# Dense experts of a PEER layer: z through one PSUM bank in two pieces, five output tiles kept in PSUM

## The chip, the cores and the metric

The kernel runs on one core of a Trainium2 chip. The metric is device time in microseconds (us). Three timed runs of the kernel before took 3194.96, 3195.38 and 3200.4 us; the median is 3195.38 us. One more execution was profiled, and every number from the trace is of that one.

## What is computed

The reference is one encoder block on 1024 tokens of width 1024: RMSNorm, a gated mixer of differential attention and a short convolution, then a PEER layer and a last RMSNorm. The change lies in the PEER layer:

```python
q = (xc @ w_query).reshape(c, PEER_HEADS, 2, PEER_HALF_DIM)
sc = jnp.einsum('chpd,hpnd->chpn', q, sub_keys)
s1, i1 = lax.top_k(sc[:, :, 0], 16); s2, i2 = lax.top_k(sc[:, :, 1], 16)
cand = s1[..., :, None] + s2[..., None, :]          # 256 candidates of a head
top, pos = lax.top_k(cand, 16)                      # 16 experts of 16384 for a token and head
g = jax.nn.softmax(top, axis=-1)
a = gelu(jnp.einsum('chkd,cd->chk', expert_u[eidx], xc))
out = jnp.einsum('chk,chkd->cd', g * a, expert_v[eidx])
```

Each token thus takes 8 x 16 = 128 of 128 x 128 experts, and an expert is one row of u and one row of v.

## The kernel before

The 1024 tokens are eight tiles of 128. The experts of the first five tiles (640 tokens, `GB`) are computed densely: for all 16384 experts, with a weight that is zero where a token did not choose the expert. The experts of the other three tiles are gathered: for each of 128 choices of a tile, an indirect DMA fetches one row of u and v for every token (`uvt`, four buffers), VectorE multiplies u with the token and sums (line 746), ScalarE takes the GELU and the weight (lines 748 and 749), and VectorE adds weight times v to `acc` (line 755): 3 x 128 = 384 such steps.

The dense part goes over the 128 rows of the expert grid, 128 experts in a row, in the loop of line 974. Matmul operands are split into a rounded high part and a low part (`split`: a cast on ScalarE, a subtraction on VectorE), and a product takes three matmuls: high x high, high x low, low x high (`passes`). A row i does this:

- `expert_in(i)`: u of the row is loaded (`raw`, a ring of three buffers that u, v and, at the end, h share) and split (`uh`, `uhl`). z is u times the 640 normed tokens: eight steps of 128 features, three matmuls each, for each of two halves of 320 tokens, so 48 matmuls of 320 columns. Both halves are one PSUM tile of two banks with one buffer. One GELU of 640 columns (line 929) makes `pr` (one buffer), VectorE multiplies it with the weights (line 930), and the product is split into `ph` and `phl`.
- `expert_out`: the output of the preceding block of two rows (`BLK`): ten tiles of 128 tokens x 512 features, six matmuls of 512 columns each (two rows, three matmuls). In program order five of the ten tiles follow z of the next block's first row, five z of its second row. The four tiles of the first two token tiles (`NR`) stay in four PSUM banks over all 128 rows (`held`). The other six go through two banks (`pout`), and VectorE adds each to `hacc` in SBUF (line 957), which starts from the residual h.
- `expert_v(i)`: v of the row is loaded and split into `vh` and `vhl` (three buffers each).

After the loop, `finish_rows` adds h to the held tiles, takes the last RMSNorm of the five token tiles and writes them out; each one needs one more buffer of the ring `raw` for the squares (`yo`). What is left of the gathers comes after that.

Eight PSUM banks are in use: two for z, two for `pout`, four for `held`.

The order on each engine isn't the program's order. The framework runs through the instructions with estimated durations, gives each engine what is ready by them, the earlier in program order first, and fixes that order; on the chip each engine runs its list in order and waits by semaphores. So z matmuls of one row and output matmuls of the preceding block lie mixed in the trace. The gathers and the top-k of the last tiles are generators that put in a step after so many us of matmul work (`tick`; `GATHER` is 2.0 us), and have their place in the program order from there.

## Time and profile before

| | |
|---|---|
| median of three runs | 3195.38 us |
| profiled execution | 3191.78 us |
| its span, first to last instruction | 3190.0 us |
| TensorE, VectorE, ScalarE, GpSimd busy | 94%, 83%, 41%, 29% of the span |
| granted TensorE clock, mean | 0.978 of full speed |
| matmuls of z, of the output | 6144, 3840 |
| dense GELUs, adds to hacc, gather steps | 128, 384, 384 |

Times in the rows are microseconds from the start of the span, unless marked ns. PE is TensorE's matmul, DVE is VectorE, ACT is ScalarE, POOL is GpSimd, SP is the engine that issues most DMAs. Matmuls are pipelined: the duration of one is longer than the time from its start to the next one's start. L905 is line 905 of the kernel; `out<-in` names what is written and read. What stands after `<-` in brackets is what ended the idle time before an instruction.

### The profile page before, as it was taken

The numbers are of one execution on the slowest core, as the hardware profiler recorded it, in microseconds if no ns is written. First come the engines' busy times: TensorE is split into PE (matmuls) and PEld (weight loads), VectorE is DVE, ScalarE is ACT, GpSimd is POOL, SyncE is SP. The second block draws the span as 40 slices with busy tenths as digits, with TensorE's granted clock in tenths as the row PEclk, the third lists the DMA queues.
The fourth block names the chain that finished last, engine by engine and source line by source line (L and its number), as shares of the span: only waits on it lengthen the run. The fifth ranks groups of instructions, "written<-read, shape, count | busy, mean of one in ns | idle before, by whom it ended". The sixth has DMA issues, their size and how long they took to land.

```text
span 3190.0 us, 45907 instructions
## 1 busy us (share of the span) xinstructions
PE 3012.1 (94%) x17551; PEld 2761.0 (87%) x17551; DVE 2646.3 (83%) x4665; ACT 1302.9 (41%) x2344; POOL 923.5 (29%) x716
## 2 busy tenths in 40 slices
PE   7999999898989879799999999999999999999994
PEld 6799998798988869789989989899889999999993
DVE  5442466378999996799999999999999999999898
ACT  3322364335567766533333333333333333333332
POOL 2310000035344444223222222223332323333333
PEclk9999999999999989899999999999999999999997
DMA  5451232555444375779878888888889999898887
GB/s 180 145 182 67 83 113 80 199 172 213 146 172 157 144 260 196 255 249 333 316 277 321 316 299 309 295 316 293 313 328 343 340 341 348 326 347 325 328 336 281
DMA packets 237549, 801.11 MB, mean 251 GB/s; under 512 B 18832, under 2 KB 123280, under 8 KB 174096
## 3 DMA queue, kind: packets, MB, share of 16 engines
q0 software_dynamic: 64704, 442.53, 37.5%
q1 hardware_dynamic: 152592, 305.30, 27.8%
q10 hardware_dynamic: 20032, 50.34, 4.1%
q8 instruction: 138, 2.26, 0.3%
q14 instruction: 83, 0.68, 0.1%
HBM read 714.74 MB, written 83.36 MB: 250 GB/s over the span
## 4 chain that ended last, share of the span: by engine, by line
PE 56%; DVE 17%; issue 11%; DMA 8%; POOL 4%; ACT 3%; SPq 0%; ACTq 0%; POOLq 0%; DVEq 0%
PE z L905 17%; PE pout L905 10%; PE held L905 6%; PE pq L228 4%; PE pg L228 4%; POOL uvt L739 3%; PE ph L228 3%; DMA uvt<-in_uv,idx 3%; DVE acc L755 2%; PE py L228 2%; PE pw L695 2%; DVE uvt L746 2%; DVE ms L714 1%; PE pv L228 1%; PE pk L228 1%
## 5 line engine op out<-in xcount | busy, mean ns | idle before, releaser
L739 POOL DMA_INDIRECT uvt<-in_uv,idx x384 | 528.1, 1375 | 1288.5 <-DVE acc L755 1011.0
L905 PE MATMUL z<-actTh,uh 128*128 128x320 f32 x2048 | 636.3, 311 | 5.5 <-ACT pr L929 4.5
L905 PE MATMUL z<-actTh,uhl 128*128 128x320 f32 x2048 | 636.5, 311 | 1.1 <-DVE uhl L898 1.1
L905 PE MATMUL z<-actTl,uh 128*128 128x320 f32 x2048 | 635.3, 310 | 0.0
L746 DVE SCALAR_TENSOR_TENSOR uvt<-uvt,hng 128x1024 f32<-128x1024 f32 x384 | 468.0, 1220 | 41.1 <-DMA uvt<-in_uv,idx 40.3
L755 DVE SCALAR_TENSOR_TENSOR acc<-uvt,wt,acc 128x1024 f32<-128x1024 f32 x381 | 487.8, 1280 | 1.3 <-ACT wt L749 1.2
L905 PEld LDWEIGHTS z<-actTh,uh 128*128 128x128 f32 x2048 | 386.0, 188 | 20.5 <-ACT pr L929 8.6
L905 PEld LDWEIGHTS z<-actTl,uh 128*128 128x128 f32 x2048 | 386.2, 189 | 10.1
L905 PEld LDWEIGHTS z<-actTh,uhl 128*128 128x128 f32 x2048 | 386.8, 189 | 8.5 <-DVE uhl L898 2.2
L905 PE MATMUL pout<-vh,ph 128*128 128x512 f32 x768 | 302.5, 394 | 23.2 <-ACT ph L896 15.0
L905 PE MATMUL pout<-vhl,ph 128*128 128x512 f32 x768 | 301.1, 393 | 0.0
L905 PE MATMUL pout<-vh,phl 128*128 128x512 f32 x768 | 300.5, 391 | 0.0
L718 POOL TENSOR_TENSOR o<-ms,wtr 128x512 f32<-128x512 bf16 x160 | 203.0, 1311 | 262.1 <-PE pw L695 123.4
L748 ACT ACTIVATE wt<-zt 128x1 f32<-128x1 f32 x384 | 77.0, 201 | 493.3 <-DVE uvt L746 493.0
L957 DVE TENSOR_TENSOR hacc<-pout,hacc 128x512 f32<-128x512 f32 x384 | 259.4, 681 | 19.6 <-PE pout L905 19.1
L185 DVE TENSOR_TENSOR wl<-wr,wh 128x2048 fp32r<-128x2048 f32 x66 | 157.9, 2392 | 117.7 <-ACT wh L184 117.7
L896 ACT CAST uh<-raw 128x1024 fp32r<-128x1024 f32 x128 | 134.3, 1049 | 193.5 <-DMA raw<-in_uT 187.9
L184 ACT CAST wh<-wr 128x2048 fp32r<-128x2048 f32 x74 | 141.0, 1907 | 168.9 <-DMA wr<-in_wq 31.6
L695 PE MATMUL pw<-o,o 128*128 128x128 f32 x1280 | 169.1, 284 | 41.2 <-POOL o L718 17.6
L695 PEld LDWEIGHTS pw<-o,o 128*128 128x128 f32 x1280 | 161.1, 198 | 49.3 <-issue 25.6
L905 PE MATMUL held<-vhl,ph 128*128 128x512 f32 x512 | 199.6, 391 | 0.0
L720 ACT CAST o<-ms 128x512 f32<-128x512 bf16 x160 | 179.6, 1138 | 38.8 <-DVE ms L714 26.0
(290 smaller groups left out, 6673.5 us busy)
## 6 DMA issues: line engine op xcount, KB each, us to landing
raw<-in_uT SPq DMA_DIRECT2D x128, 512.0 KB
raw<-in_uv SPq DMA_DIRECT2D x128, 512.0 KB
w_d<-wbuf ACTq DMA_DIRECT2D x20, 2048.0 KB
wt<-w_d SPq DMA_DIRECT2D x32, 1280.0 KB
wr<-in_wcols SPq DMA_DIRECT2D x28, 1024.0 KB
wr<-in_wq SPq DMA_DIRECT2D x24, 1024.0 KB
xt<-in_x SPq DMA_DIRECT2D x16, 512.0 KB
q_d<-qt POOLq DMA_DIRECT2D x32, 256.0 KB
```

The source lines that it names most:

```text
L184: A.copy(out=op[0][sl], in_=src)
L185: lo.tensor_sub(op[1][sl], src, op[0][sl].bitcast(F32))
L228: PE.matmul(pd, lhsT=l[a], rhs=r[b], start=i == 0 and j == 0, stop=i == n - 1 and j == len(c) - 1)
L695: PE.matmul(pw[:, u, :], lhsT=o2[:, t + u, :], rhs=o1[:, t + u, :], start=True, stop=True)
L718: PL.tensor_tensor(out=o1.rearrange("p t i -> p i t"), in0=ms[:, 0], in1=w[:, ts].unsqueeze(1).broadcast_to(sh), op=ALU.mult)
L720: A.copy(out=o2.rearrange("p t i -> p i t"), in_=ms[:, 1])
L739: PL.indirect_dma_start(out=t[:], out_offset=None, in_=uv, in_offset=bass.IndirectOffsetOnAxis(ap=sels[c][1][:, k:k + 1], axis=0))
L746: V.scalar_tensor_tensor(u, u, 1.0, st[c], op0=ALU.mult, op1=ALU.mult, accum_out=zt)
L755: V.scalar_tensor_tensor(st["acc"], v, wt, st["acc"], op0=ALU.mult, op1=ALU.add)
L896: A.copy(out=hi, in_=t)
L905: PE.matmul(ps, lhsT=lhs[k][a], rhs=rhs[k][b], start=first and k == 0 and j == 0, stop=last and k == n - 1 and j == 2)
L957: V.tensor_add(hacc[:, t - NR, ds], ps, hacc[:, t - NR, ds])
```

## The change

z of a row is no longer one tile of two banks. Each half of 320 tokens gets its own tile in one bank with one buffer, and its own GELU into its half of `pr`. Output tiles of the preceding block come after the GELU of the first half (`fill(0)`) and after the split of the product (`fill(1)`), and so four times in a block: three, two, three and two tiles. The bank that becomes free holds a fifth output tile: the first five of the ten (both halves of token tiles 0 and 1 and the first half of token tile 2) stay in PSUM, five are added to `hacc`. Token tile 2 is now half resident and half moving: its half of `hacc` starts from zero, and `finish_rows` adds both to h, which it reads back. The order of tiles alternates moving and resident.

```diff
-NR = 2
+NR = 5
@@ the pools of the last stage @@
-    hacc = hp.tile([P, NB - NR, D], F32, name="hacc")
-    held = [[ps_r.tile([P, 512], F32, name=f"held{t}{hf}") for hf in range(2)] for t in range(NR)]
+    tiles = [(t, hf) for t in range(NB) for hf in range(2)]
+    resident, moving = tiles[:NR], tiles[NR:]
+    hacc = hp.tile([P, len(moving), 512], F32, name="hacc")
+    held = [ps_r.tile([P, 512], F32, name=f"held{j}") for j in range(NR)]
@@ expert_in @@
-    def expert_in(i):
+    def expert_in(i, fill):
...
-        hs = halves(GB)
-        z = ps_z.tile([P, 2, 512], F32, name="z", tag="z")[:, :len(hs), :hs[0][1]]
-        for j, (c0, cn) in enumerate(hs):
-            passes(z[:, j, :], us, [(hh[:, k, c0:c0 + cn], hl[:, k, c0:c0 + cn]) for k in range(KD)], cn)
         p = dn.tile([P, GB], F32, name="pr", tag="pr", bufs=1)
-        A.activation(p.rearrange("p (h c) -> p h c", h=len(hs)), z, AF.Gelu)
+        for c0, cn in halves(GB):
+            z = ps_z.tile([P, cn], F32, name="z", tag="z")
+            passes(z, us, [(hh[:, k, c0:c0 + cn], hl[:, k, c0:c0 + cn]) for k in range(KD)], cn)
+            A.activation(p[:, c0:c0 + cn], z, AF.Gelu)
+            if c0 == 0:
+                fill(0)
         V.tensor_mul(p.rearrange("p (c t) -> p c t", t=WT), p.rearrange("p (c t) -> p c t", t=WT),
                      wts[b][:, :, i % WB, :])
-        return split(p, "ph", PHB, [P, GB], V)
+        ph = split(p, "ph", PHB, [P, GB], V)
+        fill(1)
+        return ph
@@ order of the output tiles, and expert_out @@
     order = []
-    while resident or moving:
-        for q in (moving, resident):
-            if q:
-                order.append(q.pop(0))
+    for j in range(max(len(moving), len(resident))):
+        order += moving[j:j + 1] + resident[j:j + 1]
+    slots = 2 * BLK
+    cuts = [-(-len(order) * j // slots) for j in range(slots + 1)]

     def expert_out(pv, vv, part, first, last):
-        n = len(order) // BLK
-        for t, hf in order[part * n:(part + 1) * n]:
+        for t, hf in order[cuts[part]:cuts[part + 1]]:
...
-            if t < NR:
-                passes(held[t][hf], lhs, rhs, 512, first, last)
+            if (t, hf) in resident:
+                passes(held[resident.index((t, hf))], lhs, rhs, 512, first, last)
             else:
                 ps = ps_v.tile([P, 512], F32, name="pout", tag="v")
                 passes(ps, lhs, rhs, 512)
-                V.tensor_add(hacc[:, t - NR, ds], ps, hacc[:, t - NR, ds])
+                to = hacc[:, moving.index((t, hf)), :]
+                V.tensor_add(to, ps, to)
@@ finish_rows @@
-            if t < NR:
-                y = raw_rows(h_d[rows, :])
-                for hf in range(2):
-                    ds = slice(hf * 512, (hf + 1) * 512)
-                    V.tensor_add(y[:, ds], held[t][hf], y[:, ds])
-            else:
-                y = hacc[:, t - NR, :]
+            y = raw_rows(h_d[rows, :]) if (t, 0) in resident else hacc[:, moving.index((t, 0)):moving.index((t, 0)) + 2, :]
+            y = y if (t, 0) in resident else y.rearrange("p j c -> p (j c)")
+            for hf in range(2):
+                ds = slice(hf * 512, (hf + 1) * 512)
+                if (t, hf) in resident:
+                    V.tensor_add(y[:, ds], held[resident.index((t, hf))], y[:, ds])
+                elif (t, 0) in resident:
+                    V.tensor_add(y[:, ds], hacc[:, moving.index((t, hf)), :], y[:, ds])
@@ the loop over rows @@
     for i in range(NK + BLK):
+        b, part = i // BLK - 1, i % BLK
+        prev = pv[:BLK], vv[:BLK]
+
+        def fill(j):
+            if b >= 0:
+                expert_out(*prev, 2 * part + j, b == 0, b == NK // BLK - 1)
+
         if i < NK:
-            pv.append(expert_in(i))
-        b, part = i // BLK - 1, i % BLK
-        if b >= 0:
-            expert_out(pv[:BLK], vv[:BLK], part, b == 0, b == NK // BLK - 1)
-            if part == BLK - 1:
-                pv, vv = pv[BLK:], vv[BLK:]
+            pv.append(expert_in(i, fill))
+        else:
+            fill(0)
+            fill(1)
+        if b >= 0 and part == BLK - 1:
+            pv, vv = pv[BLK:], vv[BLK:]
...
         if i == 1:
-            for t in range(NR, NB):
-                SP.dma_start(out=hacc[:, t - NR, :], in_=h_d[t * P:(t + 1) * P, :])
+            for j, (t, hf) in enumerate(moving):
+                if (t, 0) in resident:
+                    V.memset(hacc[:, j, :], 0.0)
+                else:
+                    SP.dma_start(out=hacc[:, j, :], in_=h_d[t * P:(t + 1) * P, hf * 512:(hf + 1) * 512])
```

## Rows read from the trace of the kernel before

**Rows 1.** The page's first part: busy time, share of the span and instructions.

```profile
PE 3012.1 (94%) x17551; PEld 2761.0 (87%) x17551; DVE 2646.3 (83%) x4665; ACT 1302.9 (41%) x2344; POOL 923.5 (29%) x716
```

**Rows 2.** Stretches: length, busy us (instructions) by engine, clock, DMA share, GB/s.

```profile
core 0: us, PE busy (x) PEld busy (x) DVE busy (x) ACT busy (x) POOL busy (x), PEclk, DMA share, GB/s
1400.00:2400.00 1000.00, 990.32 (x5483) 893.47 (x5482) 960.84 (x1551) 340.95 (x690) 289.54 (x207) 1.00 0.85 307
2600.00:3000.00 400.00, 400.00 (x2245) 365.82 (x2244) 367.65 (x465) 141.39 (x295) 124.77 (x88) 1.00 0.90 332
```

**Rows 3.** Chain that ended last, 2900 to 3190 us: start, length, engine and line.

```profile
2937.44 5.91 PE z L905 x40
...
3093.54 1.38 PE pout L905 x6
...
3098.81 2.95 PE held L905 x13
...
3144.74 1.20 DVE hacc L957 x2
```

**Rows 4.** TensorE in order of time, its last matmuls: start, length, instruction.

```profile
3145.40 0.50 PE L905 MATMUL pout<-vh,ph 128*128 128x512 f32 x1 [1.68 <-DVE hacc L957]
...
3148.07 0.39 PE L905 MATMUL pout<-vh,phl 128*128 128x512 f32 x1
```

**Rows 5.** Stretches of line 755 alone: accumulations of gathered experts on VectorE.

```profile
1400.00:2400.00 1000.00, 252.50 (x197) 1.00 0.85 307
...
3150.00:3190.00 40.00, 11.55 (x9) 0.53 0.71 262
```

**Rows 6.** Groups, 1200 to 3190 us: busy us, mean ns | idle before, releasers.

```profile
L755 DVE SCALAR_TENSOR_TENSOR acc<-uvt,wt,acc 128x1024 f32<-128x1024 f32 x381 | 487.8, 1280 | 1.3 <-ACT wt L749 1.2
...
L957 DVE TENSOR_TENSOR hacc<-pout,hacc 128x512 f32<-128x512 f32 x384 | 259.4, 681 | 19.6 <-PE pout L905 19.1
...
L896 ACT CAST uh<-raw 128x1024 fp32r<-128x1024 f32 x128 | 134.3, 1049 | 193.5 <-DMA raw<-in_uT 187.9 <-PE z L905 2.7 <-DVE sv L588 2.5
...
L896 ACT CAST ph<-pr 128x640 fp32r<-128x640 f32 x128 | 93.2, 729 | 163.3 <-DVE pr L930 162.3 <-issue 0.8
L929 ACT ACTIVATE pr<-z 128x640 f32<-128x640 f32 x128 | 90.0, 703 | 227.4 <-PE z L905 204.6 <-DVE phl L898 19.8 <-DVE uvt L746 2.7
...
L169 POOL TENSOR_TENSOR r_h<-m_h,mhalf 128x1 f32<-128x1 f32 x5 | 5.7, 1135 | 0.6 <-DVE m_h L167 0.5
```

**Rows 7.** ScalarE in order of time: start, length, instruction, wait before it.

```profile
1348.97 0.72 ACT L896 CAST ph<-pr 128x640 fp32r<-128x640 f32 x1 [13.14 <-DVE pr L930]
...
1363.19 0.71 ACT L929 ACTIVATE pr<-z 128x640 f32<-128x640 f32 x1 [1.20 <-PE z L905]
...
2342.78 0.71 ACT L929 ACTIVATE pr<-z 128x640 f32<-128x640 f32 x1 [2.53 <-DVE phl L898]
...
2525.79 0.71 ACT L929 ACTIVATE pr<-z 128x640 f32<-128x640 f32 x1 [3.86 <-PE z L905]
...
3097.47 0.71 ACT L929 ACTIVATE pr<-z 128x640 f32<-128x640 f32 x1 [5.22 <-PE z L905]
...
3155.13 1.06 ACT L174 ACTIVATE yo<-raw 128x1024 f32<-128x1024 f32 x1 [6.23 <-DMA out<-raw]
```

**Rows 8.** VectorE in order of time: the ends of the same four chains.

```profile
1369.43 0.81 DVE L898 TENSOR_TENSOR phl<-pr,ph 128x640 fp32r<-128x640 f32 x1
...
2349.23 0.81 DVE L898 TENSOR_TENSOR phl<-pr,ph 128x640 fp32r<-128x640 f32 x1
...
2531.19 0.81 DVE L898 TENSOR_TENSOR phl<-pr,ph 128x640 fp32r<-128x640 f32 x1
...
3103.11 0.81 DVE L898 TENSOR_TENSOR phl<-pr,ph 128x640 fp32r<-128x640 f32 x1
```

**Rows 9.** TensorE's waits, 1340 to 3125 us: total us, times, longest.

```profile
PE z L905 <- ACT pr L929: 2.2, 4, 0.9
```

**Rows 10.** ScalarE's waits, 1400 to 2300 us, same columns.

```profile
ACT uh L896 <- DMA raw<-in_uT: 136.1, 54, 7.4
```

**Rows 11.** SP's queue in order of time, 3138 to 3190 us.

```profile
3150.76 13.98 SPq L971 DMA_DIRECT2D out<-raw  x2
```

More of the change, by code (lines that the diff above doesn't have):

```diff
@@ L936, in expert_v @@
         return split(vr, "vh", VHB, [P, D], V)
-    resident = [(t, hf) for t in range(NR) for hf in range(2)]
-    moving = [(t, hf) for t in range(NR, NB) for hf in range(2)]
     order = []
-    while resident or moving:
-        for q in (moving, resident):
-            if q:
-                order.append(q.pop(0))
+    for j in range(max(len(moving), len(resident))):
+        order += moving[j:j + 1] + resident[j:j + 1]
+    slots = 2 * BLK
+    cuts = [-(-len(order) * j // slots) for j in range(slots + 1)]
     def expert_out(pv, vv, part, first, last):
-        n = len(order) // BLK
-        for t, hf in order[part * n:(part + 1) * n]:
+        for t, hf in order[cuts[part]:cuts[part + 1]]:
             ds = slice(hf * 512, (hf + 1) * 512)
```

## The prediction

> **What bounds the kernel now.** I read the busy shares first, then the stretches of the last stage, its groups, its waits, and the two ends of the chain that runs through one row. Over the whole run TensorE is busy 94% and VectorE 83% [rows 1]. The change lies in the dense-expert stage, the last 1850 us. There both engines are nearly full: from 1400 to 2400 us TensorE is busy 99.0% and VectorE 96.1%, from 2600 to 3000 us 100% and 91.9%, at a granted clock of 1.00, the higher of its levels (2.4 GHz) [rows 2].
>
> Busy is not pace, so I count matmuls. A steady z matmul takes 5.91/40 = 0.148 us, a pout one 1.38/6 = 0.230, a held one 2.95/13 = 0.227 [rows 3]. A row needs 48 of z and 30 of output: 7.09 + 18 x 0.230 + 12 x 0.227 = 13.95 us. From 2600 to 3000 us 2245 matmuls ran in 400 us, 0.178 each: that is this floor. From 1400 to 2400 us 5483 ran in 1000 us, where the same pace gives 5612 [rows 2]. The 129 missing ones x 0.178 = 23 us are all that TensorE loses there (a few per cent of the records can be missing, so this is an upper value). So TensorE sets the pace, VectorE is close behind it, and after TensorE's last matmul, which ends at 3148.5 us [rows 4], the span goes on to 3190.0: a tail of 41.5 us. In the tail stand nine of the 384 accumulations of the gathered experts [rows 5], and the finish of the output rows.
>
> **The change, part by part.** The sum is made against the profiled execution: 3191.78 us, 1.78 around its span; the median of the three timed runs is 3.6 higher.
>
> *TensorE's work.* Same matmuls, same shapes: 48 of 320 columns and 30 of 512 a row. Three pout tiles a row become 2.5; pout and held differ by 0.003 us a matmul, so 0.
>
> *VectorE's work.* One of ten tiles of a block leaves the copy to SBUF: 64 adds go. One is listed at 0.681 us [rows 6], but consecutive adds overlap, two in 1.20 us [rows 3], so 64 x 0.60 = 38 us of VectorE, 0.30 a row. Added: one memset of 128x512 (under one such add, 0.7 us) and two adds at the end. Not on the path by itself; it counts where VectorE holds up the end, below.
>
> *ScalarE's work.* The GELU of 640 columns takes 0.703 us; casts of 1024 and 640 columns take 1.049 and 0.729 [rows 6], 0.00083 us a column, so a GELU of 320 is 0.703 - 0.267 = 0.44 us. Twice that is 0.17 more a row, 22 us in all, on an engine that is busy 34% [rows 2]: hidden. SP's queue gets four loads of 256 KB in place of three of 512 KB at the start, and one more 512 KB read of h at the end (below).
>
> *The wait that is added.* Now a row's z pieces pass through one bank: piece 2 waits for the GELU of piece 1, and that GELU writes into "pr", of which there is one buffer, so it also waits until the split of the preceding row's product (phl) is done. Behind a late GELU on ScalarE stand the casts ph, vh and uh and the gathers' wt; behind TensorE's piece 2 stand the next output tiles. The cover is output tiles: slots of 3, 2, 3, 2 tiles, 4.11 us between the pieces and 2.74 after them. Measured from GELU to end of phl, the chain takes 10.2 us on average over the 70 rows from 1363 to 2350 us (7.1 in the first, 7.3 in the last), and 6.2 over the 42 rows from 2526 to 3104 us (6.2 in the first, 6.5 in the last) [rows 7, 8]; 37 of the 70 lie over 9.5. The new loop from GELU to GELU is that chain less 0.26, plus 0.44 for the first GELU and 24 x 0.148 = 3.55 for the second piece: 13.9 us on average in the first group and 9.9 in the second, without handovers. Against a row of 13.95 the second has 4 us of room, the first none. Handovers TensorE to ScalarE and back have no row of their own; the bound is 0 to 0.4 us each.
>
> Does a loop of 13.9 us slow the first 70 rows? Mostly the chain is long there because VectorE is late, with queued gather and top-k work in front of it, and nobody waits: TensorE waited 2.2 us for a GELU in the whole stage [rows 9]. If TensorE is held up, VectorE gets less to do and catches up. But ScalarE also stands 136 us (54 times) before a uh cast whose weights have not landed [rows 10], and a GELU behind that cast now has 3 to 4 us of cover where it had 6.9. The bounds for the 70 rows: -23 us (all that TensorE loses is won, because VectorE has 0.30 us a row less to do), and +95 us (every excess over 9.5 us in those 37 rows stalls TensorE). I take +5: what VectorE is relieved of about pays for the late casts. For the 56 rows behind them I take +2, because the loop has 4 us of room; the bounds are 0 and 28, the second as if one late cast of the earlier kind (136/54 = 2.5 us) came through in every fifth row.
>
> The Trainium skill, "PSUM — Partial Sum Buffer", "Summary: rules for kernel authors", speaks against one bank: an engine should read a bank other than the one that matmuls are writing. By that alone each of the 256 pieces would pay its GELU, 256 x 0.44 = 113 us. The trace of before has the same exclusion once a row (one z tile, one buffer) and shows 2.2 us for it, because output tiles lie between; whether 2.74 us of them still suffice no row shows.
>
> *Start.* Rows 0 and 1 have no output tiles to put between. Before, z of row 1 was finished while ScalarE stood 13.1 us for the first weights [rows 7]; now piece 2 of row 1 waits for the GELU that starts after that and comes out behind it: 3.55 + 0.44 = +4 us.
>
> *Last block.* Five tiles with a copy instead of six, evenly spaced: the last pout tile waited 1.7 us for its bank [rows 4]; -1.
>
> TensorE's last matmul thus moves by 4 + 5 + 2 - 1 = +10.
>
> *Tail.* A gathered expert costs VectorE a product and an accumulation over 128x1024 elements, the second 1.28 us [rows 6], the first of the same form; each overlaps its neighbour by 0.08 as the adds do, so 2.4 us. 38 us of VectorE are 16 of them. From 1400 to 2400 us they ran at 19.7 in 100 us [rows 5] with VectorE full, so there, with half of the adds that go, eight are won, and two more in the 10 us of delay: the nine late ones come before or shortly after the last matmul. What then ends last is the finish. Three output row tiles instead of two now read h back through the three-buffer "raw" ring, and each next one waits until the preceding one is written: 1.06 square [rows 7] + 1.14 power on POOL [rows 6] + 1.28 scaling (the accumulation's form) + 4.4 write (the write issued at 3150.76 released the next square at 3155.13 [rows 7, 11]) = 7.9 us each. The first starts some 8 us before the last matmul, since its two tiles are done before the last five; after two whole turns come the third row's 3.5, two rows that need no h and one write: -8 + 1.2 of adds + 2 x 7.9 + 3.5 + 2 x 1.28 + 4.4 = 19.5 us. With two gathered experts in between, 4.8, it is 24, the value I take; the ends are 18 and 41.5. 24 - 41.5 = -18 rounded.
>
> Sum: +10 - 18 = -8: 3183.8 in the profiled execution, and with the 3.6 us 3187.
>
> **The rivals.**
>
> *A, better: the freed VectorE time goes to TensorE.* For it: 0.30 us a row is more than the 23/70 = 0.33 us a row that is lost, nearly. Then 4 - 23 + 0 - 1 - 18 = -38: 3157.
>
> *B, the loop through z's one bank and "pr" closes (slower).* Place: rows 2 to 71, while the top-k and the gathers fill VectorE. It decides from the point where GELU to end of phl exceeds 13.95 - 3.55 - 0.44 - about 0.5 of handovers = 9.5 us. For it: the 10.2 us average and the 54 late casts. Against: the wait is elastic, and steady rows behind have 6.2. Price: a third to all of the 95 us, +32 to +95, so with the other terms +19 to +82; at half, 4 + 48 + 2 - 1 - 18 = +35: 3230. The rule of the Trainium skill's "PSUM — Partial Sum Buffer" ("Summary: rules for kernel authors") bears on the bank's half of this place; no term here is taken from it.
>
> *C, the tail stays.* The gathers hang on their four buffers and on DMA, 85 to 90% busy [rows 2], not on VectorE. For it: from 2600 to 3000 us VectorE had 8% to spare [rows 2], and nine accumulations were late all the same. Then +10 and no -18, or half of it: +1 to +10, 3196 to 3205.
>
> **How the numbers follow.** The forecast (3177 to 3196 as its own range) gets 0.42, A 0.22, B 0.26, C 0.10. From no change a measurement of this kernel can tell about 0.2%, 6.4 us: faster is below 3189, slower above 3201.8. The forecast lies 0.25 faster and 0.17 same; A is faster; B slower; C is split 0.04 and 0.06. Faster 0.47, same 0.21, slower 0.32. The range 3155 to 3235 reaches from A's value to just beyond the middle of B.
>
> **What would show it.** Right: hacc adds 320 instead of 384; TensorE's waits for a GELU below some 20 us from 1400 to 2400 us, and over 5480 matmuls there; the last matmul within 3140 to 3165 us; a tail near 24 us whose last links are squares and writes of rows, with no accumulation of the gather behind the first of them. B would show as z waiting for pr tens of us long before 2350 us and hardly after it, with a row period over 14.5 us. C would show as gathers still at 20 in 100 us and a tail near 40. The forecast is wrong in its main step if rows 2 to 71 take over 14.5 us or under 13.95 each, and in its second if the tail is not between 18 and 32 us.

## The result, and the profile after

The changed kernel takes 3328.43 us (median of four runs, 3317.97 to 3335.12), the kernel before 3195.17 us in the same comparison. The ratio is 1.0416, 95% interval 1.038 to 1.0452: 4.2% slower, where -0.3% was forecast. The profiled execution took 3325.73 us, its span 3324.0 us, 134.0 us more than before.

The page's first part and two stretches of the last stage, the lines that answer to [rows 1, 2]:

```profile
PE 3060.3 (92%) x17551; PEld 2775.1 (83%) x17551; DVE 2619.4 (79%) x4604; ACT 1320.1 (40%) x2472; POOL 943.4 (28%) x716
```

```profile
1400.00:2400.00 1000.00, 909.31 (x4835) 797.95 (x4834) 933.99 (x1509) 331.52 (x753) 325.71 (x225) 0.98 0.88 316
2600.00:3000.00 400.00, 389.13 (x2146) 351.29 (x2147) 362.48 (x457) 137.35 (x319) 132.33 (x92) 1.00 0.93 339
```

From 1400 to 2400 us 4835 matmuls ran instead of 5483, and from 2600 to 3000 us 2146 instead of 2245. VectorE, which lost 64 adds, is less busy over the whole run. Not so in the rows of the grid from 2 to 48: between their products it is busy 15.8 us of a row of 16.8, before 13.7 of 14.2, because its list has 3.46 accumulations of gathered experts from one product to the next instead of 2.74, and more of the top-k (counted in the timelines; the framework made that list). With this list such a row takes at least 15.8 us. TensorE waits more. Its waits from 1340 to 3125 us, the view of [rows 9] (there 2.2 us for the GELU):

```profile
PE z L907 <- ACT pr L930: 41.6, 58, 3.1
PE pout L907 <- ACT ph L898: 40.4, 25, 11.2
PE pout L907 <- DVE phl L900: 26.1, 19, 4.3
PE pout L907 <- DVE hacc L960: 21.4, 15, 4.1
```

z waits for the GELU in its bank, and the output tiles that were to cover this wait need a product (ph, phl) that is itself late. The page's groups, where [rows 6] has the same ones:

```profile
L907 PE MATMUL pout<-vh,phl 128*128 128x512 f32 x640 | 253.9, 397 | 26.2 <-DVE phl L900 26.1
L898 ACT CAST uh<-raw 128x1024 fp32r<-128x1024 f32 x128 | 134.4, 1050 | 330.5 <-PE z L907 322.3
L960 DVE TENSOR_TENSOR hacc<-pout,hacc 128x512 f32<-128x512 f32 x320 | 214.7, 683 | 56.2 <-PE pout L907 55.6
```

The adds to hacc are 320 now, as said. The cast of uh waited 187.9 us for its weights before; now it waits 322.3 us for z matmuls, which free its buffer. Weights are no longer late, rows are.

One row shows the loop. ScalarE, VectorE and TensorE of the changed kernel in order of time (start, length, instruction, and in brackets the wait before it):

```profile
1698.77 1.05 ACT L898 CAST uh<-raw 128x1024 fp32r<-128x1024 f32 x1 [0.21 <-PE z L907]
1699.72 0.43 ACT L930 ACTIVATE pr<-z 128x320 f32<-128x320 f32 x1
...
1705.62 0.72 ACT L898 CAST ph<-pr 128x640 fp32r<-128x640 f32 x1 [0.21 <-DVE pr L933]
1708.75 0.44 ACT L930 ACTIVATE pr<-z 128x320 f32<-128x320 f32 x1 [2.41 <-DVE phl L900]
```

```profile
1701.29 1.28 DVE L755 SCALAR_TENSOR_TENSOR acc<-uvt,wt,acc 128x1024 f32<-128x1024 f32 x1
1702.48 1.22 DVE L900 TENSOR_TENSOR uhl<-raw,uh 128x1024 fp32r<-128x1024 f32 x1
1703.62 1.22 DVE L746 SCALAR_TENSOR_TENSOR uvt<-uvt,hng 128x1024 f32<-128x1024 f32 x1
...
1704.76 0.82 DVE L933 TENSOR_TENSOR pr<-pr,wt 128x640 f32<-128x640 f32 x1
...
1707.84 0.82 DVE L900 TENSOR_TENSOR phl<-pr,ph 128x640 fp32r<-128x640 f32 x1
```

```profile
1698.57 0.31 PE L907 MATMUL z<-actTh,uhl 128*128 128x320 f32 x1
...
1700.20 0.42 PE L907 MATMUL z<-actTh,uh 128*128 128x320 f32 x1 [0.63 <-ACT pr L930]
...
1703.71 0.31 PE L907 MATMUL z<-actTh,uhl 128*128 128x320 f32 x1
1706.40 0.80 PE L907 MATMUL pout<-vh,ph 128*128 128x512 f32 x1 [2.38 <-ACT ph L898]
1706.99 0.63 PE L907 MATMUL pout<-vhl,ph 128*128 128x512 f32 x1
1707.41 0.63 PE L907 MATMUL held<-vh,ph 128*128 128x512 f32 x1
1707.84 0.63 PE L907 MATMUL held<-vhl,ph 128*128 128x512 f32 x1
...
1709.85 0.40 PE L907 MATMUL held<-vh,ph 128*128 128x512 f32 x1
1710.08 0.40 PE L907 MATMUL held<-vhl,ph 128*128 128x512 f32 x1
...
1712.83 0.31 PE L907 MATMUL z<-actTh,uh 128*128 128x320 f32 x1
```

Read it across. The last matmul of a row's piece 2 starts at 1698.57; the uh cast, freed by its end as the GELU is, stands before the GELU. The GELU ends at 1700.15, VectorE comes to the product only at 1704.76, behind gathered experts and uhl, and ends phl at 1708.66. Meanwhile piece 1 of the next row is ready (1704.0), but its GELU may not write pr before 1708.75. TensorE can't start piece 2, and the output tiles it has instead need ph, so it stands 2.38 us. They then lie in front of piece 2, which starts 3.6 us after its bank is free.

So I set out the loop from one GELU of a first piece to the next, averaged over rows 2 to 47 from such rows of the timeline: GELU 0.44, until piece 2 starts 2.09, piece 2 3.76, until its GELU 1.19, GELU 0.43, until VectorE's product 3.82, product to cast 0.85, cast to the end of phl 4.16, until the next GELU 0.14. The sum is 16.88 us, the row period there. The last term says that it is closed: in 40 of the 46 rows the next GELU starts within 0.3 us of the end of phl, in the other six at most 1.13 us behind it. In rows 84 to 125 the same terms give 14.47 us (VectorE's shares 1.40, 0.89 and 2.46), with 0.65 in the last.

The framework's order has changed with the bank. In TensorE's list none of the 248 pieces of z in rows 2 to 125 has an output matmul inside it; in the kernel before 166 have. So TensorE, too, has less to put into a wait than before.

The span's 134.0 us by where they arose, from the ends of z in both traces. Start (to the end of z of row 2): +8.9. Rows 2 to 71: 16.10 us each instead of 14.17, +133.6. From there to row 126: 14.46 instead of 14.02, +24.1. From there to TensorE's last matmul: -10.7. That matmul starts at 3303.92 instead of 3148.07 [rows 4]; behind it 20.1 us remain instead of 41.9, -21.8.

The gathers went the other way (line 755 alone, [rows 5] before): 214 accumulations instead of 197 from 1400 to 2400 us, and one after 3100 us.

```profile
1400.00:2400.00 1000.00, 275.17 (x214) 0.98 0.88 316
3100.00:3324.00 224.00, 1.28 (x1) 0.96 0.27 90
```

The tail is now the finish alone (chain that ended last: start, length):

```profile
3304.89 2.62 DMA out<-raw
3307.62 1.16 ACT yo L174 x2
3308.80 0.17 DVE m_h L167
...
3309.62 1.30 DVE raw L176
3310.93 2.66 DMA out<-raw
```

### The profile page after: what moved, and what is told of

It reads as the page before. It is cut to its first block, busy times and chain, and to the rows that moved or that the text cites. A ratio compares the mean times of both kernels' runs of the same rounds, so it can differ in the third digit from the quotient of the medians.

```text
span 3324.0 us, 46249 instructions
## 1 busy us (share of the span) xinstructions
PE 3060.3 (92%) x17551; PEld 2775.1 (83%) x17551; DVE 2619.4 (79%) x4604; ACT 1320.1 (40%) x2472; POOL 943.4 (28%) x716
## 4 chain that ended last, share of the span: by engine, by line
PE 44%; DVE 21%; issue 14%; DMA 12%; ACT 4%; POOL 4%; SPq 0%; DVEq 0%; ACTq 0%; POOLq 0%
PE z L907 11%; DMA uvt<-in_uv,idx 7%; PE held L907 6%; PE pout L907 5%; PE pg L228 4%; DVE acc L755 4%; PE pq L228 3%; DVE uvt L746 3%; POOL uvt L739 3%; PE ph L228 2%; PE py L228 2%; PE pw L695 2%; DVE hacc L960 2%; PE pk L228 1%; DVE ms L714 1%
## 5 line engine op out<-in xcount | busy, mean ns | idle before, releaser
L739 POOL DMA_INDIRECT uvt<-in_uv,idx x384 | 544.5, 1418 | 1183.5 <-DVE acc L755 831.3
L907 PE MATMUL z<-actTh,uh 128*128 128x320 f32 x2048 | 646.5, 316 | 50.5 <-ACT pr L930 48.9
L907 PE MATMUL pout<-vh,ph 128*128 128x512 f32 x640 | 261.4, 408 | 63.2 <-ACT ph L898 41.4
L907 PE MATMUL pout<-vh,phl 128*128 128x512 f32 x640 | 253.9, 397 | 26.2 <-DVE phl L900 26.1
L898 ACT CAST uh<-raw 128x1024 fp32r<-128x1024 f32 x128 | 134.4, 1050 | 330.5 <-PE z L907 322.3
L960 DVE TENSOR_TENSOR hacc<-pout,hacc 128x512 f32<-128x512 f32 x320 | 214.7, 683 | 56.2 <-PE pout L907 55.6
L907 PE MATMUL pout<-vhl,ph 128*128 128x512 f32 x640 | 254.7, 398 | 0.0
L907 PE MATMUL held<-vh,ph 128*128 128x512 f32 x640 | 252.9, 395 | 0.0
L907 PE MATMUL held<-vhl,ph 128*128 128x512 f32 x640 | 251.8, 393 | 0.0
L900 DVE TENSOR_TENSOR uhl<-raw,uh 128x1024 fp32r<-128x1024 f32 x128 | 157.8, 1233 | 98.7 <-ACT uh L898 98.5
```

What stands on the lines that cost most here:

```text
L739: PL.indirect_dma_start(out=t[:], out_offset=None, in_=uv, in_offset=bass.IndirectOffsetOnAxis(ap=sels[c][1][:, k:k + 1], axis=0))
L898: A.copy(out=hi, in_=t)
L900: eng.tensor_sub(lo, t, hi.bitcast(F32))
L907: PE.matmul(ps, lhsT=lhs[k][a], rhs=rhs[k][b], start=first and k == 0 and j == 0, stop=last and k == n - 1 and j == 2)
L960: V.tensor_add(to, ps, to)
```

## The experiments

The first expectations name three theories. T1: z's one bank, the GELU, the one pr and phl close a loop. T2: output tiles now come one piece of z behind the product that they need. T3: the uh cast, freed by the end of z, stands on ScalarE before the GELU. Ratios are against the kernel before in the same comparison. "Rows" are mean periods between ends of z in the profiled execution, first for rows 2 to 48, then 84 to 126; before they are 14.15 and 13.95 us, after 16.85 and 14.49.

**Which part of the change.** The fifth tile back to SBUF, one bank of z kept:

```diff
-NR = 5
+NR = 4
```

> The changed kernel with four output tiles kept in place of five; z still goes through one bank, and one bank stays unused. If the one bank (with the one pr buffer) makes the loss: as slow as the changed kernel or a little slower, 3320 to 3350 us, rows 2 to 48 near 17 us each. If the fifth resident tile or the new order of tiles does: 3220 to 3230, as with two z banks.

Measured: 3340.66 us, 1.0455 (1.0416 to 1.0494), rows 17.56 and 14.22. The fifth resident tile costs nothing; the one bank does.

The bank given back to z:

```diff
-NR = 5
+NR = 4
-    ps_z = pspool("ps_z", 1, left)
+    ps_z = pspool("ps_z", 2, left)
```

> The changed kernel with two banks for z, each piece in its own, and four output tiles kept in place of five; the pieces, two GELUs and the slots of output tiles stay. Theory 1: TensorE's waits for a GELU, some 57 us from 1300 to 3300 us, go, and little else: 3260 to 3280 us. Theory 2: the waits for ph and phl stay, 3280 to 3330. If the bank alone is the cause of everything: 3190 to 3200.

Measured: 3222.59 us, 1.0105 (1.0066 to 1.0145), rows 14.29 and 13.96. One bank more takes out nearly all of the rows' loss; the total lies between the values expected. VectorE's list is back at 2.74 accumulations a row. TensorE's waits, same stretch as above; the 14.6 is one wait at the start of the stage:

```profile
PE pout L907 <- ACT ph L898: 14.6, 1, 14.6
PE pout L907 <- DVE hacc L960: 4.9, 6, 1.5
...
PE z L907 <- ACT pr L930: 1.8, 4, 0.8
```

The last matmul is at 3154.9 us, close to before. What remains is that the last accumulation of the gathers comes at 3201 us, before at 3180; 10 of them stand behind the last add to hacc in VectorE's list, before 8.

The output tiles both behind the split, as the kernel before has them:

```diff
-            if c0 == 0:
-                fill(0)
...
+        fill(0)
         fill(1)
```

> The changed kernel with all five output tiles behind the split of the product, none between the two pieces of z; one bank for z and five tiles kept as in the changed kernel. Theory 2: two z pieces stand between a product and its use again, the waits for ph and phl (57 us) go: 3260 to 3280 us. Theory 1: nothing stands between the pieces, so the second waits for the GELU of the first, 128 x 0.7 us more: 3400 us, unless the order mixes older tiles in.

Measured: 3321.89 us, 1.0415 (1.0381 to 1.0449), rows 16.89 and 14.38. The framework orders by readiness, and here it gave the order of the kernel after once more: in the trace the lists of TensorE, VectorE, ScalarE and GpSimd are the same, instruction by instruction, by operation, tiles and shapes (17551, 4604, 2472 and 716). So this run doesn't test T2. It is a second measurement of the kernel after, and shows how far two of one order lie apart: 6.5 us in the median, 0.04 and 0.11 us a row.

z as before (two banks, one GELU), but the four slots of output tiles:

```diff
-NR = 5
+NR = 4
-        for c0, cn in halves(GB):
-            z = ps_z.tile([P, cn], F32, name="z", tag="z")
...
+        z = ps_z.tile([P, 2, 512], F32, name="z", tag="z")[:, :len(hs), :hs[0][1]]
...
+            if c0 == 0:
+                fill(0)
+        A.activation(p.rearrange("p (h c) -> p h c", h=len(hs)), z, AF.Gelu)
```

> z as in the kernel before (one tile of two banks, one GELU of 640 columns, four output tiles kept), but output tiles in the changed kernel's four slots: the first after the first half of z, the second after the split. Theory 2: slower than before by the waits for ph and phl, 3240 to 3260 us. Theories 1 and 3: like the kernel before, 3190 to 3200 us.

Measured: 3226.22 us, 1.0119 (1.0083 to 1.0155), rows 14.22 and 14.45, last matmul at 3179.7 us, last accumulation at 3213. The slots alone cost about 1%, late in the stage and in the gathers, not in rows 2 to 48. That is neither what T2 had (3240 to 3260 us) nor what T1 and T3 had (3190 to 3200). With one bank of z no run has the tiles in another place and all else the same: T2 stays untested there.

**Which link of the loop.** Two buffers of pr:

```diff
-name="pr", tag="pr", bufs=1
+name="pr", tag="pr", bufs=2
```

> The changed kernel with two buffers for pr in place of one, nothing else. Theory 1 (a closed loop: z's one bank, GELU, the one pr buffer, split of the product, next GELU): the GELUs' waits for phl (60 us, 72 times) go, and with them most of TensorE's waits; 3220 to 3260 us. Theory 2 (distance: output tiles now stand one z piece behind the product they need, so TensorE waits for ph and phl): no change, 3310 to 3335. Theory 3 (ScalarE's order: the cast of uh, set free by the same end of z, stands before the GELU): no change either.

Measured: 3243.18 us, 1.0157 (1.0112 to 1.0201), rows 14.77 and 14.55. 85 us of the 133 are gone with 2.5 KB a partition; the later rows don't move. In the loop's terms the next GELU now starts on average 3.26 us before phl ends, in place of 0.14 after it: the loop is open there. The order has changed too: 74 of the 248 pieces now have output matmuls inside, and VectorE has 2.83 accumulations a row. What the buffer does by itself, and what the order does that the framework makes for it, these runs don't separate; the same holds for the second bank and for the halves below. Of the runs below only the next and the one with light accumulations keep all pieces whole.

A third buffer of uh's high part, pr as in the kernel after:

```diff
-        hi = pl.tile(shape, F32R, name=tag, tag=tag, bufs=bufs)
+        hi = pl.tile(shape, F32R, name=tag, tag=tag, bufs=3 if tag == "uh" else bufs)
```

> The changed kernel with three buffers for the high part of u, so that its cast does not wait for the z that the GELU also waits for. Theory 3 (the cast set free by the same end of z goes before the GELU and makes z wait): rows 48 to 126 go from 14.5 to 14.0 us, 3270 to 3300 us in all. Theory 1 alone: 3315 to 3335.

Measured: 3322.98 us, 1.0408 (1.0359 to 1.0458), rows 16.77 and 14.52. The cast did leave the loop (z end to GELU fell from 1.19 to 0.09 us), and the other terms took the time back: the product's cast starts 1.26 us behind the product instead of 0.85, the next GELU 0.65 us after phl instead of 0.14. T3 alone isn't it.

Both, and a third uhl; the room comes from loading weights of two rows at a time instead of four:

```diff
-WB = 4
+WB = 2
-        u = split(ur, "uh", 2, [P, D], V)
+        u = split(ur, "uh", 3, [P, D], V)
-        p = dn.tile([P, GB], F32, name="pr", tag="pr", bufs=1)
+        p = dn.tile([P, GB], F32, name="pr", tag="pr", bufs=2)
```

> The changed kernel with two buffers for pr and three for uh and its low part; to make room the dense weights come two rows at a time in place of four. If the two losses are the pr loop (rows 2 to 48) and the uh cast that stands before the GELU (all rows), both go and VectorE's 38 us count: 3165 to 3200 us, all rows near 14.0. If the one bank alone costs the 0.5 us a row: 3225 to 3250 as with two pr buffers.

Measured: 3225.81 us, 1.01 (1.0064 to 1.0136), rows 14.04 and 13.99, last matmul at 3116.7 us, last accumulation at 3213 us. TensorE's waits in the whole stage come to 6.4 us:

```profile
PE pout L907 <- DVE hacc L960: 2.9, 4, 1.7
PE pout L907 <- ACT ph L898: 2.9, 5, 1.0
PE pout L907 <- DVE phl L900: 0.6, 1, 0.6
```

With one bank of z TensorE thus runs at its pace, once its neighbours have buffers (and VectorE's list 2.74 accumulations a row, as before). That this run is nevertheless 1% above the kernel before goes with its weight loads (below).

The gathers' accumulation over 32 of its 1024 columns, the others left out (an accumulation takes VectorE 54.02/220 = 0.25 us there in place of 1.29):

```diff
-                V.scalar_tensor_tensor(st["acc"], v, wt, st["acc"], op0=ALU.mult, op1=ALU.add)
+                V.scalar_tensor_tensor(st["acc"][:, :32], v[:, :32], wt, st["acc"][:, :32], op0=ALU.mult, op1=ALU.add)
```

> The changed kernel with the accumulation of the gathered experts cut to 32 of 1024 columns: it leaves out most of the sum over the gathered experts' v, and so some 1.1 us of VectorE for each of 381 steps. If rows 2 to 48 are slow because VectorE is late within the loop: they fall from 16.8 to 14.5 us, 3190 to 3230 us in all. If the loop is too long whatever VectorE does: 3300 or more.

Measured: 3217.31 us, 1.007 (1.0043 to 1.0097), rows 14.96 and 14.19. The loop's terms on VectorE fall from 3.82 to 1.79 and from 4.16 to 2.44 us, and the row by 1.9 of the 2.7 us that it had gained. VectorE is busy 12.1 us a row there instead of 15.8. Its queue is the largest part of the loss; with so much less of it 0.8 us a row are left, and the loop isn't fully open (0.55 in the last term).

pr as two tiles of 320 columns with one buffer each, each with its own product, cast and subtraction:

```diff
-        p = dn.tile([P, GB], F32, name="pr", tag="pr", bufs=1)
...
+            p = dn.tile([P, cn], F32, name="pr", tag=f"pr{len(pc)}", bufs=(1, 1)[len(pc)])
+            A.activation(p, z, AF.Gelu)
...
+        for c0, cn, p in pc:
+            pw = p.rearrange("p (c t) -> p c t", t=WT)
+            V.tensor_mul(pw, pw, wts[b][:, c0 // WT:(c0 + cn) // WT, i % WB, :])
+            A.copy(out=hi[:, c0:c0 + cn], in_=p)
+            V.tensor_sub(lo[:, c0:c0 + cn], p, hi[:, c0:c0 + cn].bitcast(F32))
```

> Kernel after with pr as two tiles of 320 columns, one buffer each, and nothing else. L with pr as its first link: most of the 120 us of rows 2 to 48 goes (14.3 to 15.0 us a row), the half microsecond of the later rows stays, because the cast of uh still stands before the GELU: total 3215 to 3260 us. If what frees pr is not the wait that counts, 3300 us or more.

Measured: 3228.99 us, 1.0098 (1.0065 to 1.0132), rows 14.74 and 13.97. Without more memory 99 us of the 133 come back, those of the later rows too, which I had expected to stay: my reason for them (the cast of uh) is refuted as a separate cause. The halves do more than free pr earlier: the first product, too, no longer needs the second GELU.

**Why the open loop didn't win.** With weights of two rows at a load, and gather steps placed earlier in the program:

```diff
-GATHER = 2.0
+GATHER = 1.7
```

> Kernel after with two buffers of pr, three of uh and uhl (weights of two rows at a load instead of four, for the room), and a gather step after 1.7 us of matmul work instead of 2.0. With the same buffers and 2.0 us TensorE's last matmul came at 3117 us, 31 us before that of the kernel before, and the span ended 105 us later, with gather steps at 3.3 to 3.5 us each. If what holds that version is only that the gathers lie too late in the program order (theory G), 1.7 brings some 15% of the 384 steps forward: last accumulation near 3130 to 3160 us, rows 14.0 to 14.3 us, total 3145 to 3185 us, faster than before. If the gathers are held by VectorE or by their four buffers instead (theory H), the last accumulation stays above 3190 us or the rows grow over 14.5 us, total 3200 us or more.

Measured: 3236.42 us, 1.0133 (1.0115 to 1.0151), rows 14.16 and 13.97, last accumulation at 3212 us. G's forecast missed. But earlier in the program wasn't earlier on the engines: behind the last add to hacc VectorE's list has 29 accumulations, as with 2.0 (8 in the kernel before). So the program's order isn't what holds them, and what an earlier place in VectorE's list would bring stays untested.

```diff
-GATHER = 2.0
+GATHER = 1.4
```

> The same with a gather step after 1.4 us of matmul work. G: the gathers end before the last matmul, the total is that of TensorE plus some 25 us, 3150 to 3180 us if VectorE has the room; more likely the rows 2 to 48 grow by 0.3 to 1 us each, because VectorE was already 96% busy there: 3160 to 3220 us. H: no earlier end of the gathers than with 1.7.

Measured: 3236.19 us, 1.0123 (1.0106 to 1.014), last accumulation at 3227 us. The lists of the four engines are those of the run with 1.7, so this is the same order measured again; its last accumulation lies 15 us apart in the two executions. On the kernel before, 1.7:

```diff
-GATHER = 2.0
+GATHER = 1.7
```

> Kernel before with a gather step after 1.7 us instead of 2.0, the control for the first run of this call. If the earlier gathers alone are worth something, the nine accumulations behind the last matmul go and the tail falls from 41 to about 25 us, total 3165 to 3185 us, unless VectorE, 96% busy from 1400 to 2400 us, makes the rows longer: then 3190 to 3230 us.

Measured: 3196.54 us, 1.0001 (0.9987 to 1.0014). The lists are those of the kernel before but for the order of five entries of VectorE's: again nothing was moved.

The kernel before with the same buffers and the small loads:

```diff
-WB = 4
+WB = 2
-        u = split(ur, "uh", 2, [P, D], V)
+        u = split(ur, "uh", 3, [P, D], V)
-        p = dn.tile([P, GB], F32, name="pr", tag="pr", bufs=1)
+        p = dn.tile([P, GB], F32, name="pr", tag="pr", bufs=2)
```

> Kernel before with the same extra buffers alone (pr two, uh and uhl three, weights of two rows at a load). If the single pr and the two uh closed the loop only because z's pieces follow each other through one bank, the kernel before has nothing to win from them: TensorE waited 2.2 us for a GELU in its whole last stage; last matmul 3140 to 3160 us, total within 15 us of before. If the buffers were worth as much without the change, the last matmul would come near 3117 us here too.

Measured: 3244.0 us, 1.0148 (1.013 to 1.0166). A miss: it was to be the same as before, and is 1.5% slower. That pointed at the loads, which the next run has alone on the kernel before:

```diff
-WB = 4
+WB = 2
```

> Kernel before with weights of two rows at a load instead of four, nothing else: the control for the price of these loads. W: the gathers fall to 19 to 20.5 in 100 us from 2400 to 3000 us, at 312 GB/s in place of 337, last accumulation 3200 to 3240 us, total 3220 to 3250 us, as with the extra buffers (3244 us). If the extra buffers did it instead (other places of instructions in the order), 3190 to 3200 us.

Measured: 3236.15 us, 1.0131 (1.011 to 1.0152), last matmul at 3118.7 us, last accumulation at 3216 us. The small loads are the price. The DMA packets from 2400 to 3000 us in this run and what its queue of loads took (packets, MB, share of the DMA engines' time), then the same for the kernel before (the queue) and for the run with pr in halves and a third uh (the packets), which load four rows:

```profile
DMA packets 86848, 187.79 MB, mean 313 GB/s; under 512 B 60016, under 2 KB 60016, under 8 KB 71408
...
q1 hardware_dynamic: 69488, 61.09, 33.6%
```

```profile
q1 hardware_dynamic: 41073, 60.77, 29.5%
```

```profile
DMA packets 60610, 202.95 MB, mean 338 GB/s; under 512 B 3765, under 2 KB 31911, under 8 KB 43334
```

and the accumulations of the same stretch in this run and in the one with halves:

```profile
2400.00:3000.00 600.00, 152.05 (x119) 1.00 0.90 313
```

```profile
2400.00:3000.00 600.00, 171.14 (x134) 1.00 0.91 338
```

Halving the loads puts 60016 packets under 512 bytes, and the queue of loads takes 33.6% of the DMA engines' time for 61 MB, before 29.5%. The Trainium skill, "DMA: Bandwidth & Descriptors", "Specifications", asks for 512 bytes at least for full rate; the trace agrees. But DMA's rate isn't why 119 gathered experts get through instead of 134 (133 in the kernel before). VectorE's waits for gathered rows, 1400 to 3100 us, in this run and in the kernel before:

```profile
DVE uvt L746 <- DMA uvt<-in_uv,idx: 6.6, 9, 1.2
```

```profile
DVE uvt L746 <- DMA uvt<-in_uv,idx: 35.4, 34, 4.0
```

It waits less, not more. What differs is its list: 29 accumulations stand behind the last add to hacc, in the kernel before 8. Why the framework, given small loads, puts them there isn't shown; its estimate of the loads would be a reason. It follows that the run with two pr and three uh must be held against these two controls (1.0148 and 1.0131), not against the kernel before: 1.01 with an interval that overlaps the second's. In one comparison, the changed kernel with these buffers (and 1.7 for 2.0) took 3236.42 us, the kernel before with them 3244.0, and the intervals overlap too. With its loop open the change neither costs nor brings anything that these runs can tell. TensorE's early last matmul there wasn't won by the buffers either: the control without them has it too (3118.7 against 3116.7 us). In the control 21.5 of the 29.4 us are there when z of row 2 ends (1341.7 instead of 1363.2 us): its first product starts at 1327.8 us, where the kernel before waits 10.4 us for the first weights and starts at 1348.1.

**Repairs without the small loads.** pr in halves as above, and a third buffer of uh's high part:

```diff
-        hi = pl.tile(shape, F32R, name=tag, tag=tag, bufs=bufs)
+        hi = pl.tile(shape, F32R, name=tag, tag=tag, bufs=3 if tag == "uh" else bufs)
```

> Kernel after with pr as two tiles of 320 columns, one buffer each, each with its own product, cast and subtraction, and a third buffer of uh (not of uhl); weights loaded four rows at a time as in the kernel after. The GELU of a row's first piece then waits only for the split of the preceding row's first piece, not for phl of the whole row, with no more memory for it. Theory L (loop: the bank is held too long because the GELU waits for pr, and behind that for the uh cast): rows 2 to 48 at 14.0 to 14.8 us in place of 16.9, later rows at 14.0 to 14.2. Theory W (the version with two pr and three uh lost its gain to the loads of weights of two rows, 256 bytes a packet: 120 gathered experts from 2400 to 3000 us in place of 134): here the gathers keep 21.5 to 23.5 in 100 us after 2400 us, last accumulation 3150 to 3190 us, total 3150 to 3200 us. If W is wrong, the gathers end at 3210 us again and the total is 3220 us or more. VectorE gets two instructions more a row.

Measured: 3221.65 us, 1.0071 (1.0048 to 1.0094), rows 14.87 and 13.92, last matmul at 3190.2 us, last accumulation at 3207 us. The gathers keep their rate, as theory W had it (134, above), but W's total of 3150 to 3200 us is missed: the run is still 0.7% over. Here it is rows 2 to 84 that are 0.2 to 0.7 us long. With two buffers of the first half of pr in addition:

```diff
-bufs=(1, 1)[len(pc)]
+bufs=(2, 1)[len(pc)]
```

> The same with two buffers of the first piece of pr, one of the second. L: as the run before or better, rows at 14.0 to 14.3 us, last matmul 3115 to 3140 us. W: total 3140 to 3195 us, faster than the kernel before or the same; not W: 3220 us or more.

Measured: 3230.0 us, 1.011 (1.009 to 1.0129), rows 14.62 and 13.95. No better. With one buffer of it again, and both groups of output tiles behind the split:

```diff
-            if c0 == 0:
-                fill(0)
...
+        fill(0)
         fill(1)
```

> Kernel after with pr in two tiles of 320 columns (own product and split), a third uh buffer, and both groups of output tiles behind the split of the row, as the kernel before orders them. The same without the last edit took 3221.65 us, rows 2 to 48 at 14.6 to 15.3 us. If the four slots hold the repaired version back (theory S; on the kernel before with z in two banks they went with +1.2%), rows 2 to 48 come at 14.0 to 14.5 us and the total at 3185 to 3205 us. If the single bank of z still does it (theory L), nothing changes: 3210 to 3230 us.

Measured: 3225.68 us, 1.0111 (1.0075 to 1.0147), rows 14.59 and 13.95. Placed so, the output tiles bring nothing (theory S had 3185 to 3205 us). At last two banks of z and four resident tiles, with pr in halves and the output tiles behind the split, so that only the two pieces of z are left of the change:

```diff
-NR = 5
+NR = 4
-    ps_z = pspool("ps_z", 1, left)
+    ps_z = pspool("ps_z", 2, left)
```

> Two banks of z and four resident tiles, pr in two tiles of 320 columns with own GELU, product and split, output tiles behind the split: of the change only the two pieces of z are left. With four slots and one pr this took 3222.59 us, rows 14.1 us, last accumulation 3201 us. Theory S: 3180 to 3200 us, no slower than the kernel before. Theory L: the same, since two banks don't close the loop; L alone, without S, expects some 3215 to 3225 us as before, the gathers ending last at 3200 us. Two more instructions of VectorE a row (estimated from 320 against 640 columns at some 0.1 us each) would add 25 us of its work.

Measured: 3210.3 us, 1.0041 (1.0021 to 1.0062), last matmul at 3150.5 us, last accumulation at 3196 us. The best of the repaired versions, above the 3180 to 3200 us of theory S, and still behind the kernel before. No version here beats it.

## Why the prediction was wrong

The step that failed is "I take +5" for rows 2 to 71, and with it the choice among the rivals. It measured +133.6 us, and also broke the upper bound of 95. The step's reason was that "what VectorE is relieved of about pays for the late casts": VectorE was to have 0.30 us a row less to do, and in rows 2 to 48 it had 2.1 us more (15.8 instead of 13.7). Rival B had the right place (rows 2 to 71, z's bank and the one pr) and a price that was too small at its highest end. What the runs put in the place of the step's reasons:

- *The loop was summed without what lies between its links.* The prediction had 13.9 us "without handovers", set beside a row of 13.95, and 0 to 0.4 us for each handover. Its terms were right: GELU to end of phl measures 9.26 us in rows 2 to 47 (10.2 less 0.26 was said), piece 2 3.76 (3.55). Missing were 2.09 us from the first GELU to piece 2 and 1.19 from piece 2 to its GELU. The first is output tiles in TensorE's list. I counted them as cover for the wait; they are also in the loop, since TensorE takes them in order, and they wait for the product that the loop delivers. The second is the uh cast. I had it late for its weights [rows 10]; in the changed kernel it is late for z and comes free exactly where the GELU does.
- *"The wait is elastic"* was argued from 2.2 us of waits in a trace whose loop was open [rows 9]. In the closed loop lateness of VectorE lengthens the row. The run with light accumulations shows that (VectorE's terms down by 3.7 us, rows by 1.9, the wait for piece 2 up by 1.5), and the run with the third uh shows that shortening one link moves the time to the others.
- *"If TensorE is held up, VectorE gets less to do and catches up"*: VectorE's list is fixed before the run, and the framework put 3.46 gather steps into a row instead of 2.74 (214 instead of 197 in 1000 us), between the links. The queue in front of the product stayed.
- *The bound of 95 us* took the chain's excess over 9.5 us from the trace of before as the worst case. It left out the two missing terms and what follows a stop: TensorE's clock. In the row above the eight matmuls behind the stop ran at a granted clock of 0.50.
- In rival A's case "0.30 us a row is more than" 0.33 is a slip; nothing hangs on it.

The term of the later rows, +2 within 0 to 28, measured +24.1, for a loop that is almost closed at 14.47 us where I had given it 4 us of room: the same missing terms. The start measured +8.9 for +4, the end of the last block -10.7 for -1; I didn't follow these two further.

The tail came as said, 20.1 us for 24, with squares and writes of rows as its last links and no gather behind the first; but by luck. Its reason was VectorE's relief, and the run with one bank and four resident tiles, which keeps all 384 adds, has a tail of 14.9 us. The stage was 156 us longer, and the gathers had this time. VectorE's 320 adds were right, and the fifth tile costs nothing. In the runs where the rows are near 14.1 us again (two banks, or the open loop) the last accumulation is at 3196 to 3227 us, later than before, though in some of them VectorE has fewer adds. Rival C's objection, that the gathers hang on something other than VectorE's relief, holds there; what they hang on is their place in VectorE's list, not DMA's rate, as the small loads show.

Shown: the single bank of z, with the order that the framework makes for it, causes the rows' loss (five against four resident tiles, one against two banks); VectorE's work between the links is 1.9 of the 2.7 us a row (light accumulations); the single pr is a link of the loop (two pr, or pr in halves). Not shown: how much a single bank would cost under the order of the kernel before. Open too: why the repaired versions with four-row loads stay 0.4 to 1.1% above the kernel before. With halves and one bank the rows themselves are still long (14.6 to 14.9 us in rows 2 to 48), and TensorE's last matmul comes at 3190 to 3204 us. With two banks it comes at 3155 and, with halves, at 3150 us, and 10 and 12 accumulations stand behind the last add to hacc instead of 8. The versions with halves have two more instructions of VectorE a row, but in rows 2 to 48 VectorE is busy 13.6 to 13.7 us a row with them, as before. And the order by itself moves things: the kernel before with the small loads ended TensorE's work at 3118.7 us, and with the extra buffers, for which it had waited 4.9 us in all, at 3144.7 us. So the rest of a per cent is hard to assign.

## What to carry to other kernels

Before a buffer is halved, write down the closed path through it, from its release to its next release, and add up everything that stands on that path on each in-order engine, the covering work and the casts freed by the same event too; if that sum is near the period, the change pays every delay of every engine on the path. Waits measured while a loop is open say nothing of what it costs once closed. Where a framework orders the instructions, look at the lists of the engines before reading a result: here three edits of the program left the order as it was and so tested nothing, and the buffers that did help changed it as well. And a control for the memory that pays for a repair is worth a run: here the smaller weight loads cost 1.3% and hid what the buffers did.

## What the runs showed of the hardware

The stop of 2.38 us in the row shown above cost more than itself. The stretch from 1706.40 to 1709.55 us (length, PE, PEld, DVE, ACT, POOL, clock):

```profile
1706.40:1709.55 3.15, 3.15 (x8) 2.50 (x8) 3.15 (x7) 0.44 (x1) 2.30 (x1) 0.50 0.82 243
```

TensorE had been at a granted clock of 1.00 until it stood (1690 to 1704 us); after the stop its 512-column matmuls start 0.42 to 0.43 us apart from the second on, and 0.23 apart from 1709.85 on. That is the lower of the two levels, 1.2 GHz. The mean of 0.98 from 1400 to 2400 us (1.00 before) corresponds to about 40 us at the lower level, estimated as 0.02 x 1000 / 0.5, so some 20 us of the stage's loss. The Trainium skill, "TensorE: Matmul & The Clock Gate", "A second HAM failure mode: psum-queue depth-cycling", describes a bf16 kernel that goes back and forth between the two levels because TensorE idles briefly between groups of matmuls while it cycles through PSUM banks; the trace agrees, with 0.50 behind the stop above and 0.98 in the mean.
